# A fourth quad per gate/up block: one low by an adding DMA, carried blocks in f32, and a head that starts from x already turned

## The chip, the cores and the metric

One core of a Trainium2 chip runs the kernel. The metric is the device time of one execution in microseconds (us). All inputs lie in DRAM at the start, and the output must lie there at the end. PE is TensorE, DVE is VectorE, ACT is ScalarE, POOL is GpSimd, and SP is SyncE, whose queue starts the weight loads.

## The reference

One layer over 256 tokens of width 2048, all in f32:

```python
h = x
f = swiglu(rmsnorm(h, ln_ffn1_pre), ffn1_gate, ffn1_up, ffn1_down)
h = h + 0.5 * rmsnorm(f, ln_ffn1_post)
mx = hybrid_mixer(rmsnorm(h, ln_mix_pre), w_in, rwkv..., pool..., w_proj_a, w_proj_b, w_out)
h = h + rmsnorm(mx, ln_mix_post)
f = swiglu(rmsnorm(h, ln_ffn2_pre), ffn2_gate, ffn2_up, ffn2_down)
h = h + 0.5 * rmsnorm(f, ln_ffn2_post)
# swiglu(x, g, u, d) = (silu(x @ g) * (x @ u)) @ d, with g, u 2048 x 5632 and d 5632 x 2048
# hybrid_mixer: p = u @ w_in (2048 x 8480); a WKV-7 scan branch and a pooling branch,
#   each projected to 2048, gated by sigmoids of p, added, and multiplied by w_out
```

## The kernel before

**Products.** Every f32 product is made of three f32r matmuls (mm3): each operand is split into a high part (an ACT cast) and a low part (a DVE subtraction), and high·high, high·low and low·high are summed in PSUM. A step of 128 rows of the weight (a k) against 128 tokens (a half h) and 512 columns is one mm3.

**The plan.** Most of the work is put in order by a small planner in the kernel's own code. `job` notes a piece of work with its engine, an assumed duration and a due time; `pe` notes a piece for PE; `run` calls `play`, which runs through time by these assumptions and issues each engine's earliest due piece. So the order on PE, ACT and DVE is written out when the kernel is built, and each engine follows it in order. Weight buffers are limited: `take` and `give` pass on four w buffers (f32 weights, tag w32) and five pairs of wH and wL (tag ws). A pool of 33 units of 4 KB per partition holds everything larger.

**Gate and up.** The 5632 columns of gate and up are worked off in 11 blocks of 512. Blocks 0 and 1 take plain products. Blocks 2 to 10 (list FAST) go through `seven`, which computes gate (f) and up (l) together from a string of letters. An f or l is a *pair*: two k of one weight against both halves, 12 matmuls, fed by `feed` (SP loads w, ACT casts wH, DVE subtracts wL). A q is a *quad*: two k of both weights at once by a scheme of seven products in place of eight, 21 matmuls, for which DVE makes sums of the weights (t13, t24 at L513 to L521) and their lows (L534), and for which sums S1 to S4 of the activations are made once (`sums`). `merge`, `plus` and `total` add the banks up (L570). The result is multiplied with silu of the gate, turned in 32x32 squares on DVE (`turn`, L786), and carried to its place by 16 small POOL DMAs (`carry`, L797); then ACT and DVE split it into high and low (L809, L813) for the down product.

**Down and post.** `post` multiplies the carried blocks with w_down, by the lists DOWN (with 7 and 8 quads) in both FFNs, and by OUT in the mixer, then normalises and adds the residual. For its quads `sums` first joins high and low of a carried block (join, L394).

**Head.** `head` starts the kernel: 12 turns (matmuls against the identity) warm PE; x comes in by rows, PE turns each 128x512 piece (`turn4`, L768), ACT and DVE split it, and the first gate product follows between the turns. The gain of the first norm is turned on PE too (L1781), and `setup_mixer` loads 11 parameter vectors as rows and turns them (L1152).

**Mixer.** Its first column block is begun in the plan (`lead`) and ended outside of it (`gemm_rest`). Its middle lies outside the plan, with PE's order written by hand (`weave`); w_proj_a's product at its end is in `pair_g` and `gemm_tok`.

Of the kernel before, what the change touches and what calls it, by code (L numbers as in the profile page):

```python
# [11 lines left out]
F32 = mybir.dt.float32  # L12
# [28 lines left out]
WARM = 12  # L41
# [5 lines left out]
FAST = {b: "fffqffqllqlll" for b in range(2, 11)}  # L47
# [7 lines left out]
ROWS = [("ln_mix_pre", 16), ("ln_ffn2_pre", 16), ("mu", 26), ("w0", 8), ("a0", 8),  # L55
        ("k_k", 8), ("k_a", 8)]
ROWS2 = [("r_k", 8), ("gn_w", 8), ("gn_b", 8), ("pool_scale", 8)]
# [18 lines left out]
class Block:  # L76
# [43 lines left out]
    def job(s, eng, dur, fn, due=0.0, deps=(), take=None, give=(), lag=None,  # L120
            rel=0.0):
        s.n += 1
        n = Node(s.n, eng, dur, fn, due, LAG[eng] if lag is None else lag, give)
        n.ready = rel if eng != "D" else rel - 10
        for d in deps:
            s.link(d, n)
        if take:
            s.asks.setdefault(take, []).append(n)
        if eng != "P":
            s.jobs.append(n)  # L130
        return n
# [14 lines left out]
    def run(s):  # L146
# [3 lines left out]
        for name, ns in s.asks.items():  # L150
            ns.sort(key=lambda n: n.due)
            wait[name] = deque(ns[CAPS[name]:])
            for n in wait[name]:
                n.left += 1
        order = deque(n for _, n in sorted(s.order, key=lambda o: o[0]))
        with s.tc.manual_schedule(engines={E.PE, E.Activation, E.DVE}):
            s.play(order, wait)
            s.stats()
        s.clk, s.order, s.asks, s.freed, s.jobs = 0.0, [], {}, {}, []

    def play(s, order, wait):

        free = dict(P=0.0, A=0.0, V=0.0, G=0.0, D=-10.0)
# [17 lines left out]
        def done(n, t):  # L181
            for name in n.give:
                if wait.get(name):
                    met(wait[name].popleft(), t)
            for k in n.kids:
                met(k, t)
# [81 lines left out]
    def feed(s, w, k, n, c0, t, hold=False):  # L268
# [3 lines left out]
        def get():  # L272
            b["w"] = s.get_w(w, k, n, c0, 512)

        def high():
            if hold:
                b["H"], b["L"] = s.unit(dt=F32R, p="kH"), s.unit(dt=F32R, p="kL")
            else:
                b["H"], b["L"] = [s.wp.tile([P, 1024], F32R, tag=g, name=s.nm(g), bufs=WS_BUFS)
                                  for g in ("wH", "wL")]  # L280
            s.nc.scalar.copy(b["H"][:, :m], b["w"][:, :m])  # L281
# [4 lines left out]
        def low():  # L286
            s.nc.vector.tensor_tensor(out=b["L"][:, :m], in0=b["w"][:, :m],  # L287
                                      in1=b["H"][:, :m].bitcast(F32), op=ALU.subtract)
        g = s.job("D", 1.75 * m / 1024, get, t - 9, take="w")
        h = s.job("A", aa(m), high, t - va(m) - aa(m) - 0.5, (g,), None if hold else "ws")  # L290
        return b, s.job("V", va(m), low, t - va(m) - 0.3, (h,), give=("w",))
# [10 lines left out]
    def gemm(s, w, c0, at, k0, k1, KT, evac, names, kd=lambda k: (), pss=None):  # L302
# [9 lines left out]
        for k in range(k0, k1, 2):  # L312
            b, l = s.feed(w, k, 2, c0, s.clk)
            e = s.pe(12 * MM, lambda k=k, b=b: do(k, b),
                     (l, *kd(k), *kd(k + 1), *(s.open(*names) if k == 0 else ())), ("ws",))
# [4 lines left out]
    def halves(s, w, c0, at, k0, k1, KT, names, pss, kd=lambda k, h: (), ends=None):  # L320

        fed, last = {}, None
        for k in range(k0, k1, 2):
            fed[k] = s.feed(w, k, 2, c0, s.clk + (k - k0) * 3 * MM, k - k0 >= 2 * WS_BUFS)
        for h in range(2):
            for k in range(k0, k1):
                b, l = fed[k // 2 * 2]

                def do(k=k, h=h, b=b):
# [3 lines left out]
                last = s.pe(3 * MM, do, (l, *kd(k, h), *(s.open(names[h]) if k == 0 else ())),  # L333
                            ("ws",) if h and k % 2 and k - k0 < 2 * WS_BUFS else ())
# [3 lines left out]
    def gemm_tok(s, w, c0, at, KT, evac, xs=None):  # L338

        pss = [s.pm.tile([P, 512], F32, tag="mm", name=s.nm("mm")) for _ in range(2)]  # L340
        ws = {}

        def do(k, h):
            (wH, wL), (xH, xL) = ws[k], at(k)
            s.mm3(pss[h], xH[:, h * P:h * P + P], xL[:, h * P:h * P + P], wH, wL,
                  k == 0, k == KT - 1)

        def keep(tiles):
            ws.update((k, (wH, wL)) for k, wH, wL in tiles)

        if xs:
            s.head(w, c0, KT, do, keep, xs)
        else:
            for k2 in range(0, KT, 4):
                keep(s.load_w(w, k2, min(4, KT - k2), c0, 512))
                for k in range(k2, min(k2 + 4, KT)):
                    do(k, 0)
                    do(k, 1)
        with s.tc.high_priority(offset=BOOST):
            for h in range(2):  # L360
                evac(h, pss[h])

    def lead(s, w, c0, at, KT, kd):
# [3 lines left out]
        s.run()  # L367
        return pss

    def gemm_rest(s, w, c0, at, KT, evac, pss):  # L370

        for k2 in range(STAG, KT, 4):
            ws = {k: t for k, *t in s.load_w(w, k2, min(4, KT - k2), c0, 512)}
            for k in range(k2, min(k2 + 4, KT)):
                for h in range(2):
                    (wH, wL), (xH, xL) = ws[k], at(k)
                    s.mm3(pss[f"f{h}"], xH[:, h * P:h * P + P], xL[:, h * P:h * P + P],
                          wH, wL, k == 0, k == KT - 1)
        with s.tc.high_priority(offset=BOOST):
            for h in range(2):  # L380
                evac(h, pss[f"f{h}"])

    def sums(s, src, sm, q0, nq, t, deps, own=None, hl=False):
# [12 lines left out]
        def four():  # L396
            x = tt["x"] if hl else src[j][:, q0 % 2 * 2:][:, :2 * nq].rearrange(
                "p (i b) t -> p i b t", b=2)
            a11, a21 = x[:, :, 0, :P], x[:, :, 0, P:]
            a12, a22 = x[:, :, 1, :P], x[:, :, 1, P:]  # L400
            f = tt["f"] = s.unit((P, 4, nq, P), F32, "sf")
            V.scalar_tensor_tensor(out=f[:, 0], in0=a21, scalar=-1.0, in1=a22, op0=ALU.mult,
                                   op1=ALU.subtract)
            V.scalar_tensor_tensor(out=f[:, 1], in0=f[:, 0], scalar=-1.0, in1=a11,
                                   op0=ALU.mult, op1=ALU.subtract)
# [3 lines left out]
        def parts():  # L409

            for n_ in ("sH", "sL"):
                if j % 2 == 0:
                    own["12" + n_] = s.unit((P, 2, 2, 2, P), F32R, n_)
                if j % 4 == 0:
                    own["4" + n_] = s.unit((P, 4, 2, P), F32R, n_)
            s3 = [u.rearrange("p (i b) t -> p i b t", b=2)[:, :, 0, P:] for u in src[j]]
            s12, s4 = [[own[m + n_] for n_ in ("sH", "sL")] for m in ("12", "4")]
# [27 lines left out]
        if hl:  # L445
            deps = (s.job("V", va(512 * nq), join, t - 6, deps, rel=t - 16),)
        a = s.job("V", 4 * va(P * nq), four, t - 4.5, deps)
# [10 lines left out]
    def seven(s, wf, cf, wl, cl, at, KT, sm, order, ev_first, ev_last, trail=0,  # L458
# [26 lines left out]
        def pair(k, w, c0, b):  # L485
            ws, l = s.feed(w, k, 2, c0, s.clk)

            def do():
# [4 lines left out]
                12 * MM, do, (l, *kd(k), *kd(k + 1), *banks(b + "0", b + "1")), ("ws",))  # L493
            return e

        def quad(q):
            k = 2 * q
            v, x = {}, {}
            t1 = s.clk
            t2, t3, t4 = [t1 + m * MM for m in (6, 9, 15)]  # L500

            def get(n_, *tiles):
                v[n_] = t = s.wp.tile([P, 1024], F32, tag="w32", name=s.nm("w32"),
                                      bufs=W32_BUFS).rearrange("p (a c) -> p a c", a=2)
# [19 lines left out]
            def split(n_, m, t, deps, give=()):  # L524
                def high():
                    wH, wL = [s.wp.tile([P, 1024], F32R, tag=g, name=s.nm(g), bufs=WS_BUFS)
                              for g in ("wH", "wL")]
                    x[n_] = [t_[:, :m * 512].rearrange("p (a c) -> p a c", a=m)
                             for t_ in (wH, wL)]
                    nc.scalar.copy(x[n_][0], v[n_])  # L530

                def low():
# [4 lines left out]
                h = s.job("A", aa(w_), high, t - va(w_) - aa(w_) - 0.5, deps, "ws")  # L537
                return s.job("V", va(w_), low, t - va(w_) - 0.3, (h,), give=give)
            ga = s.job("D", 1.75, lambda: get("a", (k, wl, cl), (k + 1, wf, cf)), t1 - 9, (), "w")
            gb = s.job("D", 1.75, lambda: get("b", (k, wf, cf), (k + 1, wl, cl)), t2 - 9, (), "w")  # L540
# [5 lines left out]
            s.job("N", 0, None, 0, (la, j2), give=("w",))  # L546
            s.job("N", 0, None, 0, (lb, j4), give=("w",))
# [6 lines left out]
                 (la, *dep, *banks("p1", "f0")), ("ws",))  # L554
            s.pe(3 * MM, lambda: mul("l0", rows(k + 1, 0), x["b"][0]),
                 (lb, *banks("l0")), ("ws",))
            s.pe(6 * MM, lambda: (mul("p5", S_(1), x["t13"][0]),
                                  mul("p7", S_(3), x["t13"][1])),
                 (l13, *banks("p5", "p7")), ("ws",))
            return s.pe(6 * MM, lambda: (mul("p6", S_(2), x["t24"][0]),  # L560
                                         mul("l1", rows(k + 1, 1), x["t24"][1])),
                        (l24, *banks("p6", "l1")), ("ws",))
        u = []
# [5 lines left out]
        def add(o, b, i):  # L569
            V.tensor_tensor(out=u[o], in0=pss[b], in1=u[i], op=ALU.add)  # L570
# [4 lines left out]
        def merge(e, t):  # L575
            j0 = s.job("A", 0.5, start, t, (e,), "u")
# [10 lines left out]
        for c in order:  # L587
# [5 lines left out]
            else:  # L593
                last[c] = pair(next(ks[c]), *wc[c], c)
# [12 lines left out]
        if trail:  # L607
# [4 lines left out]
            s.halves(wl, cl, at, KT - trail, KT, KT, ("l0", "l1"), pss, lambda k, h: kd(k), end)  # L612
# [5 lines left out]
        s.job("N", 0, None, 0, fin, give=("u",))  # L618
        return use

    def head(s, w, c0, KT, do, keep, xs):

        load, turn = xs
        w32 = {}
# [4 lines left out]
        def split(k):  # L629
            n, t = w32[k]  # L630
            keep(s.two(t, k, n, 512))
        E = mybir.EngineType
        with s.tc.manual_schedule(engines={E.PE, E.Activation, E.DVE, E.SP}):
            ps = s.psum("warm")
            for _ in range(WARM):
                s.nc.tensor.transpose(ps[:, :P], s.ident, s.ident)
            load(0, 0)
            load(1, 0)
            load(None, None)
# [1215 lines left out]
```

## Time and profile before

| | |
|---|---|
| median of 3 runs | 2032.9 us (2032.25 to 2036.04) |
| the profiled execution | 2033.49 us |
| its span, first to last instruction | 2031.8 us |
| PE busy | 2014.8 us, 99% |
| DVE busy | 1735.4 us, 85% |
| ACT busy | 1164.7 us, 57% |
| POOL busy | 326.6 us, 16% |
| DMA | 423.55 MB, mean 208 GB/s |

The profile was taken in one execution. A row of a view names the line of the kernel, the engine, the operation and the tiles it writes and reads; "x61" is a count, and behind the bar stand the busy time, the mean duration of one in ns, and the idle time of the engine just before it with what ended it. In the timeline a row begins with the start and the duration in us; in square brackets stands the idle time before it. In the table by stretches, each engine has its busy time and the number of its instructions, and at the end stand the granted clock, the share of the DMA engines and GB/s. PE's matmuls overlap: the duration of one is longer than the distance to the next.

### The profile page before, as it was taken

The numbers are of one execution on the slowest core, as the hardware profiler recorded it, in microseconds if no ns is written. First come the engines' busy times: TensorE is split into PE (matmuls) and PEld (weight loads), VectorE is DVE, ScalarE is ACT, GpSimd is POOL, SyncE is SP. The second block draws the span as 40 slices with busy tenths as digits, with TensorE's granted clock in tenths as the row PEclk, the third lists the DMA queues.
The fourth block names the chain that finished last, engine by engine and source line by source line (L and its number), as shares of the span: only waits on it lengthen the run. The fifth ranks groups of instructions, "written<-read, shape, count | busy, mean of one in ns | idle before, by whom it ended". The sixth has DMA issues, their size and how long they took to land.

```text
span 2031.8 us, 28759 instructions
## 1 busy us (share of the span) xinstructions
PE 2014.8 (99%) x10011; PEld 1664.1 (82%) x10011; DVE 1735.4 (85%) x2300; ACT 1164.7 (57%) x1559; POOL 326.6 (16%) x673
## 2 busy tenths in 40 slices
PE   9999999999999999999999999999999999999997
PEld 7888888888888888888788788888888878888886
DVE  6989999988998857789689577769999989989986
ACT  7555565555565566685575444565565555555653
POOL 0121112211000023403220111012211122110000
PEclk9999999999999999999999999999999999999999
DMA  7666676766667777757456557676666767666674
GB/s 261 205 198 218 217 220 203 226 201 221 208 207 253 233 210 215 205 176 215 144 176 183 161 171 271 209 219 192 213 211 216 222 190 232 201 221 209 205 258 146
DMA packets 226842, 423.55 MB, mean 208 GB/s; under 512 B 24063, under 2 KB 27529, under 8 KB 226697
## 3 DMA queue, kind: packets, MB, share of 16 engines
q1 hardware_dynamic: 204137, 384.70, 60.8%
q0 software_dynamic: 22272, 36.51, 5.5%
q8 instruction: 78, 1.28, 0.3%
q10 hardware_dynamic: 288, 0.52, 0.1%
q14 instruction: 67, 0.55, 0.1%
HBM read 396.69 MB, written 8.39 MB: 199 GB/s over the span
## 4 chain that ended last, share of the span: by engine, by line
PE 97%; issue 1%; DMA 1%; DVE 1%; ACT 1%; POOL 0%; DVEq 0%; POOLq 0%; SPq 0%; ACTq 0%
PE mm L264 27%; PE mm L266 27%; PE mm L265 27%; PE ms L266 4%; PE ms L265 4%; PE ms L264 4%; PE tr L768 1%; DMA x<-T 0%; PE pA L1575 0%; PE mc L728 0%; PE pU L1671 0%; DMA w<-in_ffn_gate_dram 0%; PE pSa L1683 0%; PE pY L1706 0%; PE pT L1742 0%
## 5 line engine op out<-in xcount | busy, mean ns | idle before, releaser
L264 PE MATMUL mm<-wH,xH 128*128 128x512 f32 (+1 forms) x2232 | 871.6, 391 | 0.0
L266 PE MATMUL mm<-wH,xL 128*128 128x512 f32 (+1 forms) x2232 | 866.5, 388 | 0.6 <-DVE xL L777 0.5
L265 PE MATMUL mm<-wL,xH 128*128 128x512 f32 (+1 forms) x2232 | 866.6, 388 | 0.2
L281 ACT CAST wH<-w 128x1024 fp32r<-128x1024 f32 x373 | 388.1, 1053 | 231.3 <-PE mm L266 139.5
L287 DVE TENSOR_TENSOR wL<-w,wH 128x1024 fp32r<-128x1024 f32 x373 | 449.4, 1221 | 77.8 <-ACT wH L281 72.0
L266 PEld LDWEIGHTS mm<-wH,xL 128*128 128x128 f32 x2232 | 419.0, 188 | 87.9 <-DVE xL L777 2.3
L264 PEld LDWEIGHTS mm<-wH,xH 128*128 128x128 f32 x2232 | 419.1, 188 | 86.4 <-ACT xH L772 0.2
L265 PEld LDWEIGHTS mm<-wL,xH 128*128 128x128 f32 x2232 | 419.3, 188 | 85.1 <-DVE wL L287 1.0
L530 ACT CAST wH<-t 128x1024 fp32r<-128x1024 f32 x172 | 181.1, 1053 | 221.9 <-DVE t L521 113.1
L797 POOL DMA_DIRECT2D x<-T x352 | 173.1, 499 | 735.2 <-issue 299.0
L241 DVE TENSOR_TENSOR wL<-w,wH 128x1024 fp32r<-128x1024 f32 (+3 forms) x178 | 209.9, 1188 | 82.7 <-ACT wH L240 81.2
L240 ACT CAST wH<-w 128x1024 fp32r<-128x1024 f32 (+3 forms) x178 | 182.1, 1027 | 149.7 <-PE mm L266 129.3
L534 DVE TENSOR_TENSOR wL<-t,wH 128x1024 fp32r<-128x1024 f32 x172 | 205.9, 1219 | 14.3 <-ACT wH L530 13.6
L530 ACT CAST wH<-w 128x1024 fp32r<-128x1024 f32 (+1 forms) x172 | 143.1, 834 | 70.7 <-PE mm L266 32.5
L534 DVE TENSOR_TENSOR wL<-w,wH 128x1024 fp32r<-128x1024 f32 (+1 forms) x172 | 163.7, 952 | 5.2 <-ACT wH L530 5.0
L513 DVE TENSOR_TENSOR t<-w,w 128x1024 f32<-128x1024 f32 x86 | 105.0, 1220 | 12.2 <-DMA w<-in_ffn_down_dram 7.6
L570 DVE TENSOR_TENSOR u<-mm,u 128x512 f32<-128x512 f32 x92 | 61.1, 683 | 11.0 <-PE mm L266 11.0
L265 PE MATMUL ms<-wL,sH 128*128 128x512 f32 x174 | 67.9, 390 | 1.4 <-DVE wL L534 1.4
L264 PE MATMUL ms<-wH,sH 128*128 128x512 f32 x174 | 67.8, 390 | 1.0 <-ACT wH L530 1.0
L266 PE MATMUL ms<-wH,sL 128*128 128x512 f32 x174 | 67.7, 389 | 0.0
L570 DVE TENSOR_TENSOR u<-ms,u 128x512 f32<-128x512 f32 x92 | 61.3, 687 | 1.6
L809 ACT CAST xH<-x 128x512 fp32r<-128x512 f32 x44 | 26.8, 617 | 62.4 <-DMA x<-T 59.5
(332 smaller groups left out, 2064.4 us busy)
## 6 DMA issues: line engine op xcount, KB each, us to landing
w<-in_w_in_dram SPq DMA_DIRECT2D x128, 512.0 KB
w<-in_ffn_up_dram SPq DMA_DIRECT2D x122, 512.0 KB
w<-in_ffn_gate_dram SPq DMA_DIRECT2D x120, 512.0 KB
w<-in_ffn_down_dram SPq DMA_DIRECT2D x116, 512.0 KB
w<-in_ffn_down_dram SPq DMA_DIRECT2D x120, 256.0 KB
w<-in_ffn_gate_dram SPq DMA_DIRECT2D x112, 256.0 KB
w<-in_ffn_up_dram SPq DMA_DIRECT2D x108, 256.0 KB
w<-in_w_out_dram SPq DMA_DIRECT2D x28, 512.0 KB
```

What stands on the lines that cost most here:

```text
L240: s.nc.scalar.copy(vH, v)
L241: s.nc.vector.tensor_tensor(out=vL, in0=v, in1=vH.bitcast(F32), op=ALU.subtract)
L264: nc.tensor.matmul(ps, aH, bH, start=start, stop=False)
L265: nc.tensor.matmul(ps, aH, bL, start=False, stop=False)
L266: nc.tensor.matmul(ps, aL, bH, start=False, stop=stop)
L281: s.nc.scalar.copy(b["H"][:, :m], b["w"][:, :m])
L287: s.nc.vector.tensor_tensor(out=b["L"][:, :m], in0=b["w"][:, :m], in1=b["H"][:, :m].bitcast(F32), op=ALU.subtract)
L513: V.tensor_tensor(out=v["t13"], in0=v["a"], in1=v["b0"].to_broadcast([P, 2, 512]), op=ALU.subtract)
L530: nc.scalar.copy(x[n_][0], v[n_])
L534: V.tensor_tensor(out=L, in0=v[n_], in1=H.bitcast(F32), op=ALU.subtract)
L570: V.tensor_tensor(out=u[o], in0=pss[b], in1=u[i], op=ALU.add)
L797: nc.gpsimd.dma_start(out=x[0][q * 32:q * 32 + 32, i], in_=src[i * 32:i * 32 + 32, q])
```

## The change

FAST goes from 3 quads and 10 pairs to 4 quads and 8 pairs per block, in blocks 2 to 10 of both FFNs. A capital letter marks a pair whose low is made another way (`feed_add`): ACT writes −w, rounded as wH is, to wL, and a POOL DMA adds w onto it in place; DVE has no part in it:

```diff
-FAST = {b: "fffqffqllqlll" for b in range(2, 11)}
+WARM = 26
+AHEAD = 9.0
+MORE=(dict(w=(400,)*2, ws=(400,)*3), dict(w=(550,)*2, ws=(550,)*3))
+FAST = {b: "Ffqffqlqqlll" for b in range(2, 11)}

+    def feed_add(s, w, k, c0, t):
+        b = {}
+        def get():
+            b["t"] = s.get_w(w, k, 2, c0, 512, b["w"] is not None)
+        def high():
+            b["H"], b["L"] = s.room(b["ws"] is not None)
+            s.nc.scalar.copy(b["H"], b["t"])
...
+        def minus():
+            s.nc.scalar.activation(out=b["L"], in_=b["t"], func=AF.Copy, scale=-1.0)
+        def add():
+            s.nc.gpsimd.dma_start(out=b["L"], in_=b["t"], accum_op=ALU.add)
+        g = s.job("D", 1.75, get, t - AHEAD - 9, take=("w", b))
+        h = s.job("A", aa(1024), high, t - AHEAD, (g,), ("ws", b))
+        m = s.job("A", aa(1024), minus, t - AHEAD + 0.1, (h,))
+        a = s.job("G", 0.93, add, t - AHEAD + 1.5, (m,), lag=0.0)
+        return b, s.job("D", 3.2, lambda: None, t - AHEAD + 2, (a,), give=(("w", b),))
```

MORE lends the plan units as further buffers, two for w and three pairs for wH and wL, up to 400 us of planned time in FFN1 and 550 us in the plan that holds FFN2.

The carried blocks stay in f32 (list hX, one unit each in place of two): `carry` ends with the DMAs, the split into high and low becomes a job of `post`, due just ahead of the block's first use, and `sums` reads hX without a join. The S sums use plain adds and subtractions, with the sign of S1 turned, and their tiles are kept under a block number:

```diff
+        if hX is not None:
+            return s.job("N", 0, None, 0, ms)
+        return s.split(lambda: x[0], hT, b, t + 10.5, (ms,))
...
+            for b, t in sorted(first.items(), key=lambda a: a[1]):
+                hj[b] = s.split(lambda b=b: hX[b], hT, b, t - (8.5 if b * 2 < n else 2.5),
+                               ((xj[b],),), t - 22)
```

The host lays x out a second time with its 2048 columns on the partitions (x_t) and all parameter vectors as columns (cols). `head` loads x_t, splits each k with one ACT and one DVE instruction of 256 columns, and warms PE with 26 turns; x by rows is loaded after that, for the statistics of the first norm alone:

```diff
-            turn(0, 0)
-            split(1)
-            turn(1, 0)
...
+        def part(k):
+            H, L = [u[:, k % 4] for u in uT[k // 4]]
+            v = xT[k // 4][:, k % 4]
+            nc.scalar.activation(out=H, in_=v, func=AF.Copy, scale=g[:, k:k + 1])
+            nc.vector.scalar_tensor_tensor(out=L, in0=v, scalar=g[:, k:k + 1],
+                                           in1=H.bitcast(F32), op0=ALU.mult,
+                                           op1=ALU.subtract)
```

In the mixer `lead` now holds its whole column block, and w_proj_a's product, its gating and its turns (`plan_pa`) become jobs of the second plan, which counts ACT and DVE as taken for its first 3 us. The norms' statistics are jobs too (`stat`). The scan's tile t11 is laid out by group.

627 lines of the change are left out of this document (314 added, 313 removed).

## The prediction

> **What bounds the kernel now.** I read the page first.
>
> ```profile
> span 2031.8 us, 28759 instructions
> PE 2014.8 (99%) x10011; PEld 1664.1 (82%) x10011; DVE 1735.4 (85%) x2300; ACT 1164.7 (57%) x1559; POOL 326.6 (16%) x673
> PE 97%; issue 1%; DMA 1%; DVE 1%; ACT 1%; POOL 0%; DVEq 0%; POOLq 0%; SPq 0%; ACTq 0%
> ```
>
> PE is busy 99% of the span and carries 97% of the chain that ended last. So time falls only if PE executes fewer instructions or waits less. The busy times by stretch show what a gate/up block costs (the first row has the head and blocks 0 and 1, 138 to 388 us lies in blocks 3 to 8, the third row is in the down product):
>
> ```profile
> 0.00:98.00 98.00, 95.58 (x430) 78.45 (x431) 75.28 (x112) 61.80 (x102) 12.23 (x52) 1.00 0.72 233
> 138.00:388.00 250.00, 250.00 (x1104) 207.09 (x1103) 238.25 (x272) 145.42 (x166) 47.15 (x96) 1.00 0.69 215
> 475.00:697.00 222.00, 222.00 (x981) 183.80 (x981) 195.90 (x230) 124.61 (x146) 12.09 (x24) 1.00 0.68 221
> ```
>
> 1104 matmuls in 250 us: one of 512 columns costs 0.2266 us of PE. The third busy column, DVE, has 238.25 of 250 us, 95%: there the next bound is close. ACT has 58%, DMA 0.69.
>
> **The change, part by part.** *The fourth quad.* A quad does with 21 matmuls what two pairs do with 24. A block goes from 3×21 + 10×12 = 183 matmuls (41.5 us) to 4×21 + 8×12 = 180 (40.8 us). Nine blocks in each of two FFNs: 18 × 3 × 0.2266 = 12.2 us less PE. What this costs DVE comes from the timeline, where one quad's work stands in line:
>
> ```profile
> 152.26 1.22 DVE L513 TENSOR_TENSOR t<-w,w 128x1024 f32<-128x1024 f32 x1
> 153.40 1.22 DVE L534 TENSOR_TENSOR wL<-w,wH 128x1024 fp32r<-128x1024 f32 x1
> 154.53 0.68 DVE L517 TENSOR_TENSOR t<-w,t 128x512 f32<-128x512 f32 x1
> 155.13 0.68 DVE L534 TENSOR_TENSOR wL<-w,wH 128x512 fp32r<-128x512 f32 x1
> 155.74 0.68 DVE L521 TENSOR_TENSOR t<-w,t 128x512 f32<-128x512 f32 x1
> 156.34 1.22 DVE L534 TENSOR_TENSOR wL<-t,wH 128x1024 fp32r<-128x1024 f32 x1
> ```
>
> Start to start, 1024 columns take 1.14 us and 512 take 0.60. A quad is four of the first (t13 and three lows) and three of the second: 6.36 us. A pair's low is 1.14. Beside them a block has 8 sums of banks, 2 products and 2 turns (512 columns each), and today 2 lows of a carried block. Before: 19.1 + 11.4 + 14×0.60 = 38.9 us; the row above gives 0.953 × 41.5 = 39.5, so 0.6 us are bubbles. After: 4×6.36 + 7×1.14 (the F pair's low goes to a DMA) + 12×0.60 = 40.6 us, or 41.2 with the bubbles, against 40.8 us of PE. DVE goes from 95% to about 100% of PE's time.
>
> Whether PE then waits depends on DVE's idle time. Today, in 138 to 388 us:
>
> ```profile
> L287 DVE TENSOR_TENSOR wL<-w,wH 128x1024 fp32r<-128x1024 f32 x61 | 73.6, 1221 | 6.2 <-ACT wH L281 4.5
> L534 DVE TENSOR_TENSOR wL<-t,wH 128x1024 fp32r<-128x1024 f32 x36 | 42.9, 1220 | 1.3 <-ACT wH L530 1.2
> L513 DVE TENSOR_TENSOR t<-w,w 128x1024 f32<-128x1024 f32 x18 | 22.0, 1220 | 1.8 <-DMA w<-in_ffn_gate_dram 1.7
> L813 DVE TENSOR_TENSOR xL<-x,xH 128x512 fp32r<-128x512 f32 x12 | 8.3, 688 | 2.1 <-ACT xH L809 2.1
> ```
>
> 11.75 us of idle in six blocks, 1.95 each. The L287 part is mostly full buffers (its casts wait for PE to free wH), which is slack and not a cost; L813's goes with the carried lows. 1.3 and 1.8 us stay, 0.5 per block. So DVE falls behind by between 0 and 0.9 us a block (40.6 to 41.2, plus 0 to 0.5, less 40.8). Nine blocks make 0 to 8 us per FFN, 0 to 16 in all. Against it stand the stock of ready weights at the start of block 2 (five wH/wL buffers, now up to eight with MORE; one is 2.7 us of PE in a pair) and the two extra w buffers. I take 1.5 us of waits per FFN, +3 in all: near the low end, because the first blocks and the down product leave DVE room to fill and empty the stock. The sums for the fourth quad are made once per FFN, in blocks 0 and 1, where DVE has 75 of 98 us.
>
> ```profile
> L281 ACT CAST wH<-w 128x1024 fp32r<-128x1024 f32 x373 | 388.1, 1053 | 231.3 <-PE mm L266 139.5
> ```
>
> ACT gets 1.5 casts more per quad than per two pairs, and the F pair's negation of the same size: 2.6 us a block at this row's 1.05, less the two carried highs, on 17 us of idle per block. Hidden.
>
> *Carried blocks in f32.* Their high/low splits leave the gate/up blocks. Today these make PE wait twice, once per FFN:
>
> ```profile
> 409.09 0.62 ACT L809 CAST xH<-x 128x512 fp32r<-128x512 f32 x1 [5.57 <-DMA x<-T]
> 410.91 0.40 PE L264 MATMUL ms<-wH,sH 128*128 128x512 f32 x1
> 411.98 0.50 PE L265 MATMUL ms<-wL,sH 128*128 128x512 f32 x1 [0.67 <-DVE wL L534]
> 414.05 0.40 PE L266 MATMUL mm<-wH,xL 128*128 128x512 f32 x1
> 1643.95 0.62 ACT L809 CAST xH<-x 128x512 fp32r<-128x512 f32 x1 [6.86 <-DMA x<-T]
> 1644.22 0.39 PE L266 MATMUL ms<-wH,sL 128*128 128x512 f32 x1
> 1645.57 0.50 PE L264 MATMUL ms<-wH,sH 128*128 128x512 f32 x1 [0.96 <-ACT wH L530]
> 1648.90 0.40 PE L266 MATMUL mm<-wH,xL 128*128 128x512 f32 x1
> ```
>
> ACT stood 5.6 and 6.9 us at a cast whose carry DMA was late, with the quad's wH casts behind it. From 410.91 to 414.05 lie 8 matmul steps (1.81 us) in 3.14; from 1644.22 to 1648.90 lie 9 (2.04) in 4.68: 1.3 + 2.6, 4.0 us lost, which go. The splits come back at the down product, 9 blocks × 2 × 0.60 = 10.8 us of DVE less four joins (4×1.14), 6 us on its 26 us of idle in 222: hidden if the carries have landed, and all but the last two have had a block's time.
>
> *The adding transfer.* One 512 KB DMA from POOL in each of 18 blocks, issued by plan 7.5 us ahead of the pair that needs it. No such add is in the trace; the nearest are POOL's plain transfers:
>
> ```profile
> x<-T POOLq DMA_DIRECT2D x352, 32.0 KB, 3.9
> h<-hsp POOLq DMA_DIRECT2D x8, 512.0 KB, 9.2
> gb<-in_ln_ffn_post_dram POOLq DMA_DIRECT2D x4, 512.0 KB, 5.7
> xr<-in_x_dram POOLq DMA_DIRECT2D x4, 512.0 KB, 6.7
> ```
>
> 5.7 to 9.2 us for the size. At 5.7 or 6.7 it lands before PE asks (cost 0, my value: h and xr are issued four at once and share the engines, gb stands nearly alone); at 9.2 it is 1.7 us late, 18 × 1.7 = 31 us. It queues on POOL behind carry moves only if a carry is late; ACT's casts are in front of it and ACT has room. [...]
>
> *The head.* The rows, in order of time:
>
> ```profile
> 1.72 2.82 PE L636 MATMUL warm<-ident 128*128 128x128 f32 x12 [1.72 <-POOL ident masks.py:199]
> 5.62 0.62 ACT L240 CAST wH<-w 128x512 fp32r<-128x512 f32 x1 [2.60 <-DMA w<-in_ffn_gate_dram]
> 5.99 1.12 PE L768 MATMUL tr<-ident,x 128*128 128x128 f32 x4 [0.18 <-DMA x<-in_x_dram]
> 6.75 0.78 PE L264 MATMUL mm<-wH,xH 128*128 128x512 f32 x1
> 22.51 0.60 PE L768 MATMUL tr<-ident,x 128*128 128x128 f32 x4
> 22.86 0.48 PE L264 MATMUL mm<-wH,xH 128*128 128x512 f32 x1
> 23.18 0.39 PE L265 MATMUL mm<-wL,xH 128*128 128x512 f32 x1
> 33.12 0.40 PE L264 MATMUL mm<-wH,xH 128*128 128x512 f32 x1
> ```
>
> The 96 matmuls of gate block 0 run from 6.75 to 33.12, 26.4 us for 21.8 us of work. Six groups of four turns stand between them (22.51 to 23.18 is 0.67 for 0.23: 0.44 each, 2.6); 1.9 are waits and slow first matmuls. With x coming in already turned, both go, but for 0.3 I keep. The start hangs on the first weight (5.62) and on 26 warming turns in place of 12. In these rows a turn takes 0.21 us as late as 6.5 us ((2.82−0.42)/11; four in 1.12), so 26 of them from 1.72 would end at 7.3 if none is faster; with the later half at twice the speed, 5.9. I take 6.8, near the slow rows. 6.8 + 21.8 + 0.3 = 28.9: 4.2 us gained, 3.7 to 5.1. [...] The two turns by which setup_mixer brings its gain columns to the partitions go too (0.1 us each by the spacing of late turns, 0.44/4). The gains and the first step of x go out on ACT's queue, the rest of x on SP's between the weights. The x rows for the statistics (2 MB more) queue on SP behind x and w, ahead of block 0's up weights.
>
> ```profile
> 2.00:24.00 22.00, 21.31 (x100) 17.03 (x100) 13.87 (x33) 14.43 (x37) 1.74 (x22) 1.00 1.02 366
> ```
>
> Loads run at 366 GB/s in these 22 us; x, w, x again and the first up weights are 8.5 MB, 23 us, so they are there before 29: hidden. A step k needs 384 KB in 1.36 us of PE, 289 GB/s: also covered.
>
> *The rest.* lead's remainder and the w_proj_a product move from the tile scheduler into the plan: the same matmuls, turns and DMAs in another order, POOL's msp loads 25 to 30 us ahead of their use. The S sums by plain adds, tiles kept by block number, statistics as planned jobs and the other layout of t11 keep the number and width of their instructions; normed in FFN1 has one scaling of x in place of an add and a product, in blocks 0 and 1 on DVE's room. PE's chain has 97% of the span, so there is little to win in all of this, and I cost it 0; the nearest bound for a loss is one late ACT cast, 1.3 to 2.6 us (above).
>
> Sum, against this execution's own 2033.5 us (span 2031.8; 0.6 over the median 2032.9): 2033.5 − 12.2 − 4.0 − 4.2 − 0.2 + 3 = 2015.9, say **2016**.
>
> **The rivals.** *DVE becomes the bound.* The stock does not help and DVE's shortfall, 0.5 to 0.9 us a block, is paid by PE in full: waits of 8 to 16 us in all, 2012.9 + 8 to 16, so 2021 to 2029. If DVE kept today's whole idle of 1.95 us, a block would take 42.6 to 43.2 us, over the 41.5 of now, and the time would be 2033.5 − 8.4 + 18 × 1.1 to 1.7, 2045 or more. For it: the 95% above; no row shows DVE held at 100% for long. Against: most of today's idle is full buffers.
>
> *The add is late (the other side).* Each F pair opens its block, so a late landing stops PE at once, and quads behind it give no slack. Every microsecond of lateness costs 18. It decides at 17.5/18 = 1.0 us late, a landing 8.5 us after issue; at 9.2 us the time is 2016 + 31 = 2047. For it: the h row, the destination that must be read as well as written, 0.69 DMA share. Against: gb and xr rows, and ACT's room to issue earlier.
>
> *The carry stall only moves.* The splits wait at the head of the down product for late carries and stop ACT there as at 1644: 4 us or twice that again, 2020 to 2024.
>
> **How the numbers follow.** Forecast (PE still the bound, waits of 0 to 8 us, 2011 to 2021): 0.60. DVE the bound: 0.22 (0.18 for 2021 to 2029, 0.01 within 0.2% of before, 0.03 above). Add late: 0.09 (0.08 slower, 0.01 no change). Carry stall moved: 0.09. A measurement of this kernel tells 0.2%, 4 us, from no change. Faster 0.60 + 0.18 + 0.09 = 0.87; same 0.02; slower 0.11. The range: down to 2010 (no waits give 2012.9, the head's best another 0.9, the rest the run's own spread of 2 us), up to 2028, nearly all of the DVE case. Left out: the rest of it, the late add and a little below, 0.18.
>
> **What would show it.** Right: 512-column matmuls down by 54; gate block 0's 97th such matmul near 29 us; no ACT wait on a carry DMA before the down product; gate/up blocks of 40.8 us with DVE at 97% or more; PE's waits there under 8 us. Wrong: PE waiting at a block's first pair on a DMA (the add); PE waiting on wL all through the blocks (DVE); long ACT waits after 460 us (the carries).

## The result and the profile after

The changed kernel takes 2014.4 us (median of 4 runs, 2014.3 to 2015.2), the kernel before 2032.6 beside it: ratio 0.9908, interval 0.9891 to 0.9925. The profiled execution has a span of 2012.8 us, 19.0 less than before. The top of its page, with the chain by engine:

```profile
span 2012.8 us, 28601 instructions
PE 1997.0 (99%) x9936; PEld 1651.9 (82%) x9936; DVE 1764.8 (88%) x2362; ACT 1200.2 (60%) x1599; POOL 339.8 (17%) x689
...
PE 97%; DVE 1%; issue 1%; ACT 1%; DMA 0%; SPq 0%; POOL 0%; DVEq 0%; POOLq 0%; ACTq 0%
```

PE is still the bound. Busy time by stretch (length, then PE, PEld, DVE, ACT, POOL with their counts, granted clock, DMA share, GB/s): head with blocks 0 and 1; six gate/up blocks of FFN1; the down product; the nine blocks of FFN2, but for the first 8 us and with the first 9 of its down product.

```profile
0.00:96.00 96.00, 93.52 (x412) 77.95 (x413) 74.08 (x105) 62.54 (x88) 12.89 (x51) 1.00 0.83 286
135.00:385.00 250.00, 250.00 (x1104) 207.07 (x1104) 248.97 (x291) 151.84 (x172) 52.75 (x102) 1.00 0.76 236
463.00:700.00 237.00, 237.00 (x1055) 196.31 (x1054) 216.89 (x274) 141.48 (x190) 15.73 (x30) 1.00 0.68 223
1412.00:1780.00 368.00, 368.00 (x1625) 304.84 (x1624) 360.96 (x421) 228.76 (x263) 76.64 (x150) 1.00 0.72 223
```

DVE is busy 248.97 of 250 us, 99.6%, and PE waits for nothing in that stretch: 250.00 busy. The view of PE's waits for the whole execution is short (us in total, times, longest):

```profile
PE warm L649 <- POOL ident masks.py:199: 1.7, 1, 1.7
PE mm L274 <- DVE wL L250: 0.8, 1, 0.8
PE pS L1712 <- ACT R L1706: 0.7, 1, 0.7
PE mm L275 <- DVE xL L759: 0.3, 1, 0.3
```

The splits of the carried blocks, in the groups of ACT, first before and then after the change (the last columns are ACT's idle time ahead of them and its releaser):

```profile
L809 ACT CAST xH<-x 128x512 fp32r<-128x512 f32 x44 | 26.8, 617 | 62.4 <-DMA x<-T 59.5 <-DVE wL L534 2.9
```

```profile
L803 ACT CAST xH<-x 128x512 fp32r<-128x512 f32 x44 | 25.4, 615 | 1.0 <-issue 1.0
```

44 casts either way; ACT stood 59.5 us at them for carry DMAs, and no longer does.

The 19.0 us come apart so. 54 matmuls of 512 columns fewer are recorded (8328 for 8382): 12.2. Call it a gap when the starts of two such matmuls lie further apart than 0.227 us, and count what is over. These gaps fell by 1.35 us in 400 to 450 and by 2.67 in 1600 to 1650, the places of the two carry stalls: 4.0. The head, to the 97th such matmul (30.51 for 33.12): 2.6. Together 18.8. The shares are read off the two traces by place; no run puts the carried blocks or the head back alone.

### The profile page after: what moved, and what is told of

The parts are those of the page before. It is cut to its first block, busy times and chain, and to the rows that moved or that the text cites. A ratio compares the mean times of both kernels' runs of the same rounds, so it can differ in the third digit from the quotient of the medians.

```text
span 2012.8 us, 28601 instructions
## 1 busy us (share of the span) xinstructions
PE 1997.0 (99%) x9936; PEld 1651.9 (82%) x9936; DVE 1764.8 (88%) x2362; ACT 1200.2 (60%) x1599; POOL 339.8 (17%) x689
## 3 DMA queue, kind: packets, MB, share of 16 engines
HBM read 398.79 MB, written 8.39 MB: 202 GB/s over the span
## 4 chain that ended last, share of the span: by engine, by line
PE 97%; DVE 1%; issue 1%; ACT 1%; DMA 0%; SPq 0%; POOL 0%; DVEq 0%; POOLq 0%; ACTq 0%
PE mm L273 27%; PE mm L275 26%; PE mm L274 26%; PE ms L275 5%; PE ms L274 5%; PE ms L273 5%; PE pA L1596 0%; PE tr L750 0%; DMA w<-in_ffn_gate_dram 0%; PE mc L732 0%; DVE fg L1052 0%; PE pU L1692 0%; DVE wL L298 0%; DVE xL L759 0%; PE pSa L1704 0%
## 5 line engine op out<-in xcount | busy, mean ns | idle before, releaser
L273 PE MATMUL mm<-wH,xH 128*128 128x512 f32 (+1 forms) x1711 | 668.8, 391 | 0.0
L274 PE MATMUL mm<-wL,xH 128*128 128x512 f32 (+1 forms) x1711 | 663.2, 388 | 0.8 <-DVE wL L250 0.8
L275 PE MATMUL mm<-wH,xL 128*128 128x512 f32 (+1 forms) x1711 | 663.4, 388 | 0.3 <-DVE xL L759 0.3
L292 ACT CAST wH<-w 128x1024 fp32r<-128x1024 f32 x251 | 262.6, 1054 | 174.8 <-PE mm L275 122.9
L298 DVE TENSOR_TENSOR wL<-w,wH 128x1024 fp32r<-128x1024 f32 x251 | 301.3, 1218 | 58.3 <-ACT wH L292 56.7
L250 DVE TENSOR_TENSOR wL<-w,wH 128x1024 fp32r<-128x1024 f32 (+2 forms) x159 | 188.2, 1192 | 74.4 <-ACT wH L249 73.0
L249 ACT CAST wH<-w 128x1024 fp32r<-128x1024 f32 (+2 forms) x159 | 162.7, 1027 | 135.6 <-PE mm L275 113.6
L273 PE MATMUL mm<-kH,xH 128*128 128x512 f32 x449 | 175.5, 391 | 0.0
L275 PE MATMUL mm<-kH,xL 128*128 128x512 f32 x449 | 174.9, 389 | 0.0
L274 PE MATMUL mm<-kL,xH 128*128 128x512 f32 x449 | 174.7, 389 | 0.0
```

The lines of the kernel that those rows point to most:

```text
L249: s.nc.scalar.copy(vH, v)
L250: s.nc.vector.tensor_tensor(out=vL, in0=v, in1=vH.bitcast(F32), op=ALU.subtract)
L273: nc.tensor.matmul(ps, aH, bH, start=start, stop=False)
L274: nc.tensor.matmul(ps, aH, bL, start=False, stop=False)
L275: nc.tensor.matmul(ps, aL, bH, start=False, stop=stop)
L292: s.nc.scalar.copy(b["H"][:, :m], b["t"][:, :m])
```

## Experiments: what lets DVE run full without PE waiting

Two theories for the gate/up blocks. One: DVE's work, 40.6 us in a block of 40.8, just fits, the spare wH/wL pairs level out the rest, and the F pair's transfer is needed to make it fit. The rival: the stock gained in the first blocks carries a DVE that is too slow, and the lent buffers matter little.

**Four quads alone.** The kernel before with only the new list, its F written as a plain pair:

```diff
-FAST = {b: "fffqffqllqlll" for b in range(2, 11)}
+FAST = {b: "ffqffqlqqlll" for b in range(2, 11)}
```

> The kernel before with four quads and eight plain pairs in blocks 2 to 10 and nothing else of the change (carried blocks split in the gate/up blocks, no adding transfer, no lent buffers, old head). Theory: DVE's work per block is 40.6 + 1.14 + 2 x 0.60 = 43.0 us, 2.2 over PE's, 20 us per FFN, of which a stock of 4 to 8 us is saved: 2032.6 - 12.2 + 24 to 32, so 2044 to 2052, slower than before. Rival (quads pay by themselves): 2020 to 2022.

Measured 2082.0 us, ratio 1.0241 (1.0225 to 1.0256): the right direction, several times the size. Its blocks 3 to 8 and PE's longest waits:

```profile
135.00:385.00 250.00, 243.55 (x1047) 194.34 (x1046) 249.23 (x290) 146.17 (x168) 46.90 (x96) 1.00 0.67 209
```

```profile
PE mm L265 <- DVE wL L534: 17.1, 34, 1.5
PE ms L265 <- DVE wL L534: 11.8, 42, 0.9
```

1047 matmuls in 250 us make 43.0 us for a block of 180. DVE's work there is 40.6 + 1.14 (the F pair's low) + 1.20 (two carried lows) = 42.9. So here DVE is the bound, and PE pays the difference from the start; the stock that I had credited was not there. The shortage runs on into the last block, which alone has 6.8 us of gaps, and into the down product from 494 us on, with 3.8.

**The F pair by DVE, all else as changed.**

```diff
-FAST = {b: "Ffqffqlqqlll" for b in range(2, 11)}
+FAST = {b: "ffqffqlqqlll" for b in range(2, 11)}
```

> The changed kernel, but the first pair of each block takes its low on DVE again (F becomes f, no adding transfer). Theory (PE's instructions set the time as long as DVE's work per block is under PE's 40.8 us; what is over is paid, less a stock of ready weights): DVE is busy 243.97 of 245 us in blocks 3 to 8 of the changed kernel, 40.6 us per block; with 1.14 more it is 41.8, 1.0 over PE, 9 us per FFN. With 4 to 8 us of stock 1 to 5 us per FFN are paid: 2016 to 2024, with PE waiting on DVE late in the gate/up blocks. Rival (DVE's load is not the limit, the add is not needed): 2014 to 2015. Second rival (no stock): 2032.

Measured 2024.8 us, 0.9967 (0.9954 to 0.998). Blocks 3 to 8, and PE's waits:

```profile
135.00:385.00 250.00, 249.83 (x1101) 206.36 (x1100) 249.51 (x289) 144.74 (x163) 46.99 (x96) 1.00 0.67 213
```

```profile
PE tr L750 <- DVE sga L1352: 4.7, 1, 4.7
PE ms L274 <- DVE wL L534: 2.1, 7, 0.6
```

DVE is full (99.8%) and PE still hardly waits up to 341 us: the stock lasts for six blocks. In the last three PE loses 0.7, 0.9 and 1.8 us, and 0.5 behind them: 3.9 us in FFN1 and 4.2 in FFN2. That is the theory's stock, seen at work, and the add's worth in the blocks: 8 us. The wait of 4.7 from 1224 us on lies far from the blocks, at w_proj_a's turns; that the list alters the order of the second plan there is my reading. The granted clock is 0.50 for 6.8 us about it (1225.96 to 1232.78), and this execution took 2028.0 us, 3.2 over the median. Nothing in my theories had that.

**No buffers lent.**

```diff
-        s.run(MORE[0])
+        s.run()
...
-        s.run(MORE[1], 3.0)
+        s.run({}, 3.0)
```

> The changed kernel without the lent buffers (MORE empty in both plans; four w buffers and five wH/wL pairs throughout). Theory: DVE's work is just under PE's in a block, so no deep stock is needed: 2014 to 2018. Rival (the lent buffers are what lets DVE run at 100% without PE waiting): 2020 or more, with PE waits spread over the blocks.

Measured 2076.6 us, 1.0214 (1.0198 to 1.023): 62 us over the changed kernel. My theory fell. Its blocks, with DVE's largest idle group:

```profile
135.00:385.00 250.00, 241.00 (x1037) 192.65 (x1036) 237.87 (x275) 144.53 (x161) 51.76 (x101) 1.00 0.71 217
```

```profile
L298 DVE TENSOR_TENSOR wL<-w,wH 128x1024 fp32r<-128x1024 f32 x39 | 47.1, 1220 | 12.0 <-ACT wH L292 12.0
```

DVE is no longer full: it stands 12.0 us at lows whose casts are late, while PE waits for those lows. That a DVE with this much to do is not the bound but is itself starved was in neither theory. Two kinds of buffer were taken away at once, so each was then lent alone.

**The three pairs alone**, without the two staging buffers w:

```diff
-MORE=(dict(w=(400,)*2, ws=(400,)*3), dict(w=(550,)*2, ws=(550,)*3))
+MORE=(dict(ws=(400,)*3), dict(ws=(550,)*3))
```

> The changed kernel with only the three extra wH/wL pairs lent in the gate/up blocks, and not the two extra staging buffers w (both kinds lent: 2014.4 us; neither: 2076.6). Theory (an F pair holds its w from the load to the landing of its add, some 20 us, and takes it from the four others, so that loads come late): most of the 62 us come back, 2045 to 2075, with ACT waiting on the DMA of w and DVE waiting on ACT. Rival (the three pairs are what carries DVE's shortfall): 2014 to 2025.

Measured 2083.4 us, 1.0255 (1.0235 to 1.0275): the pairs by themselves bring nothing (7 us more than with nothing lent). The blocks, and ACT's idle time there, which names what is missing:

```profile
135.00:385.00 250.00, 235.12 (x1011) 190.60 (x1010) 231.56 (x268) 142.40 (x159) 51.81 (x101) 0.99 0.70 211
```

```profile
L530 ACT CAST wH<-w 128x512 fp32r<-128x512 f32 (+1 forms) x36 | 28.2, 797 | 25.0 <-DMA w<-in_ffn_up_dram 14.6 <-DMA w<-in_ffn_gate_dram 8.8 <-PE ms L275 1.5
...
L292 ACT CAST kH<-w 128x1024 fp32r<-128x1024 f32 x21 | 21.9, 1047 | 16.1 <-DMA w<-in_ffn_up_dram 15.5 <-DMA w<-in_ffn_gate_dram 0.5
L292 ACT CAST wH<-w 128x1024 fp32r<-128x1024 f32 x17 | 17.9, 1051 | 13.0 <-DMA w<-in_ffn_up_dram 11.9 <-DMA w<-in_ffn_gate_dram 1.2
```

Over 50 us of ACT's time in six blocks go on weights that have not come, at a DMA share of 0.70, less than the 0.76 at which the changed kernel has no waits: not the rate of the DMA engines holds them, but loads that start late for want of a buffer. ACT's wait alone would not say so: with four quads alone it waits some 36 us for weights too, while DVE is full. Here DVE is not: it is busy 231.56 of 250 us.

**The two w alone** (and, in the same kernel, the head's third load halved; that part is told below):

```diff
+MORE=(dict(w=(400,)*2), dict(w=(550,)*2))
```

> The changed kernel with two edits that act in different stretches of the trace. In the head: the weights of k = 2 and 3 as two loads of 256 KB with casts and lows of their own, and 22 warming turns, without the tiny loads (the up weight stays first on SP's queue). In the gate/up blocks: only the two extra staging buffers w lent, and not the three extra wH/wL pairs (pairs alone gave 2083 us). Head, theory (the stall at 10.3 to 11.5 us comes from the arrival and the splitting of one load of 1024 columns; the mended order before this one only lost its gain by late up weights): first matmul at 6.7 to 7.2, no stall over 0.3 us before the up block, 97th matmul at 29.0 to 29.6; rival (a later weight stalls instead): 30.0 or later. Blocks, theory (the two w buffers are what the F pair takes away, and a stock of ready pairs is not needed): no waits of PE on wL between 96 and 460 us, 2012.8 to 2013.6 in all; rival (the pairs are the stock that carries a DVE at 99.6%): waits of PE on wL of 1 to 2 us a block, 2025 to 2050.

Measured 2026.5 us, 0.9969 (0.9957 to 0.998). Blocks 3 to 8 and the main wait:

```profile
135.00:385.00 250.00, 248.95 (x1092) 204.21 (x1091) 246.60 (x288) 155.69 (x171) 52.71 (x102) 1.00 0.76 232
```

```profile
PE ms L274 <- DVE wL L534: 3.0, 10, 0.5
```

With w alone the blocks lose 9 us over both FFNs (4.3 and 5.0 more between starts than in the changed kernel), about half a microsecond a block. Of the other 3 us over the changed kernel most lie at 1200 to 1250 (1.8) and in the altered head (0.3). So of the lent buffers the two w are worth some 50 us (2076.6 to 2026.5, with the altered head in it) and the three pairs, on top of them, some 9. Both theories had a part of it: the pairs carry a shortfall of the size that I had worked out (0.5 to 0.9 a block), and without the w there is nothing to carry. An F pair keeps its w from its load to the landing of its add, which may be why two more are needed; no run tries that by itself. The first run of this section points the same way: with plain pairs and four w buffers DVE was full (249.23) at 43.0 us a block, and in the changed kernel with nothing lent it stood idle (237.87) at 43.4. But those two differ in the carried blocks and the head as well.

**The old list in the changed kernel.**

```diff
-FAST = {b: "Ffqffqlqqlll" for b in range(2, 11)}
+FAST = {b: "fffqffqllqlll" for b in range(2, 11)}
```

> The changed kernel with the old list of three plain quads and ten plain pairs in blocks 2 to 10; head, f32 carried blocks and lent buffers stay. Theory: 54 matmuls of 0.2266 us come back, 12.2 us, and nothing else: 2026.6, within 1. Rival (part of the gain comes from elsewhere or the quads cost something): more than 1.5 us off that, under 2025 or over 2028.

Measured 2033.8 us, 1.0006 (0.9996 to 1.0015), 7 over the forecast and no faster than the kernel before: span 18.9 over the changed kernel's. 12.2 of it is the quads. New waits of PE hold the rest, and they eat up what the head and the carried blocks had gained:

```profile
PE tr L750 <- DVE sga L1352: 3.1, 1, 3.1
...
PE ms L274 <- DVE wL L534: 1.5, 1, 1.5
...
PE mm L274 <- DVE wL L298: 0.7, 1, 0.7
```

The last two and the matmuls about them cost 3.3 us at 1814 to 1820, early in the down product of FFN2, which begins near 1788; the first costs 3.1 up to 1229, and 1.3 more in slower matmuls behind it. The carry stalls at 411 and 1644 are not there, so the changed kernel is without them under either list.

**Eight quads in the down product.** Two pairs of its first column group made a quad:

```diff
-DOWN = ((0, "fffffffffqffffqfflqlllqllqllqllqlllll", 0),
+DOWN = ((0, "ffffffffqffffqffqlqlllqllqllqllqllll", 0),
```

> The changed kernel with an eighth quad in the first column group of each down product (one quad for two pairs: 3 matmuls of 512 columns less, twice): 6 x 0.2266 = 1.36 us less PE; DVE has idle time there (217 of 237 us busy). Theory (PE is the bound there and the quad's lows hide): 2013.1, 8322 matmuls of 512 columns recorded for 8328. Rival (the changed list shifts the plan's order and opens waits elsewhere, as with the other lists tried): 2014.4 or more, with the waits named in PE's view.

Measured 2014.8 us, 0.991 (0.9896 to 0.9923). The six matmuls went (8322 recorded), and the profile shows a new wait at 536.6 us:

```profile
536.58 0.50 PE L274 MATMUL ms<-wL,sH 128*128 128x512 f32 x1 [1.20 <-DVE wL L534]
```

With what is around it, it costs 2.0 us for 1.4 gained. The rival had it; the 0.4 us between the medians lies within the spread of the runs.

**A shorter lead for the adds.**

```diff
-AHEAD = 9.0
+AHEAD = 3.0
```

> The changed kernel with the planned lead of the adding transfers cut by 6 us (AHEAD 9.0 to 3.0). In the changed kernel the adds were issued 11 to 12 us ahead of the F pair that reads them and took 6.7 to 7.3 us to land, so the slack is about 4 to 5 us. Theory (the add costs nothing only because it is issued early; each us of lateness costs 17 to 18 us over the two FFNs): issued some 5.5 us ahead, it lands 1.2 to 1.8 us late at each of 17 blocks, 20 to 31 us in all, 2035 to 2046 us, with waits of 1 to 2 us of PE on kL or wL at the first pair of the blocks. Rival one (PE's order holds other ready work, or the plan's engines still run ahead of their due times): within 0.2% of 2014. Rival two (the later lead also frees the w buffer and the wH/wL pair later, or earlier, so that DVE's supply shifts): waits on wL in the midst of the blocks rather than at their first pair.

Measured 2020.7 us, 0.9942 (0.9927 to 0.9956), 6 over the changed kernel: outside the theory and outside the first rival, but nearer to the rival. The adds go out only 2 to 5 us later, since ACT runs ahead of its due times. The answer on the add's line (its landings), first of the changed kernel and then of this one, with PE's wait on it:

```profile
DMA to landing us min/median/max: 5.4/7.0/9.2
```

```profile
DMA to landing us min/median/max: 5.1/8.1/9.8
```

```profile
PE mm L274 <- DMA wL<-w: 0.4, 1, 0.4
```

One add, issued at 331.73 us, took 9.8 us, and PE stood at its low until 341.55. In the changed kernel the adds are issued 11 to 12 us ahead (124.72 for a pair that PE reaches at 136.9), so 9.2 does no harm; the landings spread wider than the 6.7 to 7.3 of the expectation. Here the lead is 8 to 10 in the blocks after the first, and the slowest just shows. Of the 6 us, 2.3 lie in the mixer (850 to 900) and 1.8 at 1800 to 1850, in FFN2's down product, away from the adds, and 0.7 at this one.

## Experiments: the head

The head gained 2.6 us and not 4.2. The changed kernel's rows, in order of time:

```profile
0.81 0.44 SPq L235 DMA_DIRECT2D w<-in_ffn_up_dram  x1
...
1.30 0.47 SPq L235 DMA_DIRECT2D w<-in_ffn_gate_dram  x1
...
1.72 5.81 PE L649 MATMUL warm<-ident 128*128 128x128 f32 x26 [1.72 <-POOL ident masks.py:199]
...
7.18 0.71 PE L273 MATMUL mm<-wH,xH 128*128 128x512 f32 x1
...
9.17 1.05 ACT L249 CAST wH<-w 128x1024 fp32r<-128x1024 f32 x1 [0.83 <-DMA w<-in_ffn_gate_dram]
...
10.27 0.50 PE L273 MATMUL mm<-wH,xH 128*128 128x512 f32 x1
...
11.53 0.50 PE L274 MATMUL mm<-wL,xH 128*128 128x512 f32 x1 [0.76 <-DVE wL L250]
...
30.51 0.39 PE L273 MATMUL mm<-wH,xH 128*128 128x512 f32 x1
```

The first load on SP's queue is an up weight that PE wants at 30 us; the 26 turns hold PE to 7.2; the third weight (k = 2 and 3, one load of 512 KB) lands at 9.17, its low is ready at 11.5, and PE loses 1.0 us there. Theories: the up weight, the turns, or the loads as a whole.

**Tiny loads to hold the up weights back**, ahead of the loads of the columns and of x by rows, with 26 turns and then with 20:

```diff
+            for _ in range(W32_BUFS):
+                hold = s.wp.tile([P, 1024], F32, tag="w32", ...)
+                nc.sync.dma_start(out=hold[:, :8], in_=s.cols_in[:, :8])
             x(None, None)
```

> The changed kernel with four tiny loads (8 columns each) put into the four staging buffers of weights in the head, so that no up weight can be fetched ahead of the first gate weights; in the changed kernel one up weight of 512 KB, wanted at 30 us, was the first load on SP's queue. Theory (that load holds up the first gate weights and causes the second stall of 0.5 us at 11.5 us): the first gate weight lands 0.5 to 1.2 us earlier; the first matmul stays at 7.2, since the 26 warming turns end at 7.3, but the stall at 11.5 goes, and the 97th matmul of 512 columns starts near 29.9 instead of 30.5: 2013.8. Rival (the engines share bandwidth and the up weight costs the head nothing): 97th matmul at 30.4 to 30.6, 2014.4.

> The same as the run before it, with 20 warming turns in place of 26. Theory (with the first gate weight there earlier, the 26 turns at 0.21 us are what holds the first matmul): turns end at 1.72 + 20 x 0.213 = 6.0, the first matmul starts at 6.0 to 6.4, and the 97th at 28.9 to 29.3, which is what was forecast for the head; 2012.9. Rival (the first weight is the bound, or fewer turns leave the first matmuls at half rate): 97th matmul at 29.9 or later.

Measured 2018.5 us, 0.9932 (0.9918 to 0.9947), and 2020.0 us, 0.9936 (0.9922 to 0.9951). First matmul at 6.12 and 5.88. The up weight did hold the start: the kernel with eight quads has the changed head, its turns sped up as early as here (4.89 us, here 5.01), and it starts at 6.93, on a cast:

```profile
6.93 0.50 PE L273 MATMUL mm<-wH,xH 128*128 128x512 f32 x1 [0.62 <-ACT wH L249]
```

In the changed kernel's own execution no turn sped up, and there the turns hold it to 7.18. But the third weight was cast at 9.06 and 8.69, PE stood at the same place, and the 97th matmul came at 34.30 and 35.19. The tiny loads wait for their buffers on SP, and everything behind them waits too. In the kernel with 20 turns they are issued from 11.32 to 15.65 us, and the load of the columns goes out at 16.66, in the changed kernel at 11.54:

```profile
21.63 0.18 DVE L1155 TENSOR_SCALAR omu<-cols 128x27 f32<-128x27 f32 x1 [5.27 <-DMA cols<-in_cols_dram]
...
23.06 0.80 PE L274 MATMUL mm<-wL,xH 128*128 128x512 f32 x1 [3.54 <-DVE wL L250]
```

A small DVE instruction on the late columns held the weights' lows behind it. What these two tested is thus mixed with a stall of their own.

**12 turns.**

```diff
-WARM = 26
+WARM = 12
```

> The changed kernel with 12 warming turns, as before the change, in place of 26. Theory (the turns' number decides how fast the first matmuls of 512 columns run, and 26 of them also hold the first one up): the turns end at 4.3, the first matmul starts when its low is there, 6.7 to 6.8, and the first four or five matmuls take 0.34 to 0.58 us from start to start, as before the change, in place of 0.23, 0.8 to 1.0 us lost: 97th matmul at 30.5 to 31.0, 2014.4 to 2015. Rival (PE's rate after a pause of 2.4 us stays at half for some 3.4 us of work): 1.7 us lost and 0.4 won, 31.8, 2015.7.

Measured 2015.2 us, 0.9915 (0.9898 to 0.9932), 97th matmul at 30.53. The first matmul starts at 6.51; eight run at half rate (0.427 us from start to start, over 3.41 us at a granted clock of 0.50); and the block ends where it did with 26 turns, because the stall at the third weight takes up what they lost. The runs that leave the head as it is say the same: over the changed kernel and six of them the first matmul starts between 6.76 and 7.19 and the 97th between 30.26 and 30.63. The turns are not what the head hangs on.

**The third weight in two halves**, the tiny loads behind columns and x, 20 turns:

```diff
-            get(2, 2)
+            get(2, 1)
+            get(3, 1)
...
             split(2)
             part(3)
+            split(3)
```

> The changed kernel with the head's loads in another order: the four tiny loads that keep up weights away now stand behind the loads of the columns and of x (where they held nothing else up), the weights of k = 2 and 3 come as two loads of 256 KB with two casts and two lows of 512 columns in place of one of 1024, and 20 warming turns. Theory (the head is bound by the arrival and splitting of its third weight, which came at 8.7 to 9.2 us in all four orders run so far and reached PE, low included, at 11.0 to 11.5): landing half a load earlier (0.6 us), a cast of 0.62 for 1.05 and a low of 0.69 for 1.22, so the stall before 11.5 us shrinks from 1.0 to between 0 and 0.3; the first matmul starts near 6.0, the 97th at 28.5 to 29.3 in place of 30.5: 2012.4 to 2013.2. Rival (the loads as a whole are too slow: the stall only moves to the next weights): 97th at 30.0 to 30.5, 2014 to 2014.4.

Measured 2018.6 us, 0.9929 (0.9915 to 0.9942). Gate block 0 does end earlier, its 96th matmul starting at 29.43 where the changed kernel has 30.28; then the up weights, which queue behind the tiny loads (issued from 21.37 on, for 18.44), are not there:

```profile
29.43 0.39 PE L275 MATMUL mm<-wH,xL 128*128 128x512 f32 x1
31.81 0.50 PE L273 MATMUL mm<-wH,xH 128*128 128x512 f32 x1 [2.00 <-ACT wH L292]
33.07 0.50 PE L274 MATMUL mm<-wL,xH 128*128 128x512 f32 x1 [0.76 <-DVE wL L298]
```

With the up weight first again (the two-w kernel above, 22 turns) the 97th matmul starts at 30.85: the stall only moves to k = 4, whose weights land at 12.22. In the changed kernel the DMA share over this stretch is

```profile
0.00:31.20 31.20, 28.72 (x126) 24.29 (x127) 18.67 (x30) 19.08 (x30) 2.79 (x32) 1.00 0.97 358
```

Every order tried gave the first microsecond back to a load that came later. That the loads as a whole are the head's bound fits all of it; a head with fewer bytes, which would show it, was not run. No version here beats the changed kernel.

## Why the prediction came out right, point by point

- *The fourth quad, −12.2:* 54 matmuls fewer, blocks of 40.8 us, as worked out; with the old list the kernel loses another 7 us to waits in the mixer and in FFN2's down product, which the sum had not. DVE's 40.6 us a block held: 248.97 busy in 250.
- *New PE waits, +3 (0 to 16):* measured 0. DVE's bubbles, which I had at up to 1.1 us a block from the idle time before, shrank to 0.17 (1.03 in 6.1 blocks); with nothing lent they are 2.1 (12.13 in 5.8). I had put the levelling down to the stock of pairs; the runs put some 9 us on the pairs and some 50 on the w, which I had named in half a sentence.
- *Carried blocks, −4.0:* 4.0, and ACT waits on no carry DMA at all. The rival that the stall moves to the down product did not happen.
- *The adding transfer, 0:* right in the sum, though not by the reason first given. The planned lead of 7.5 us would have been short of some landings (5.4 to 9.2); the real lead was 11 to 12, for the reason that I gave second, ACT's room to issue earlier. The rows from which I priced it are medians, and I left out one of the same size, `gb<-in_ln_mix_post_dram` at 10.2; single h transfers took up to 13.8. By the planned lead those would have been late; that no add was rests on the real lead, which the sum had not sized. There the value 0 had luck.
- *The head, −4.2 (3.7 to 5.1):* 2.6; the mis-sized step. The start came at 7.18 for 6.8, at the slow end: no turn of this execution ran at full rate (each took 0.21 us), as one may or may not (last section). Behind it lie 1.6 us of waits and slow matmuls for 0.3: I had called the loads covered because their mean rate (366 GB/s) was above the need (289), and did not ask when the third weight would land.
- *The rest, 0:* the gaps between 600 and 1400 us make 104.6 us before and 103.6 after, and the end behind the last matmul of 512 columns grew by 1.1: in sum nothing.
- *Sum:* 2015.9 forecast for this execution, 2014.5 measured: waits 3 too high, the head's end 1.6 too early. The two misses partly cancel, so the sum is nearer than its terms.

## What to carry to other kernels

Where the second engine is as full as the bound, ask what keeps it fed before how much stock it has: here two staging buffers decided 50 us and three ready pairs 9. A transfer that holds its source until it lands takes that buffer out of turn (the adds here for 5 to 9 us), so price the buffer with the transfer; how much of the 50 us comes from that is not shown. And check a start by when each load lands, one by one, rather than by the mean rate.

## What the runs showed of the hardware

PE's half rate could be seen switching. In the kernel with 12 turns, four stretches of 3.41 us:

```profile
1.22:4.63 3.41, 2.82 (x12) 2.42 (x12) 0.29 (x1) 1.49 (x2) 2.20 (x25) 1.00 0.71 221
4.63:8.04 3.41, 1.31 (x4) 0.86 (x5) 2.04 (x4) 2.61 (x5) 0.00 (x0) 1.00 1.02 375
8.04:11.45 3.41, 3.41 (x10) 2.64 (x8) 2.05 (x4) 1.88 (x4) 0.00 (x0) 0.50 1.04 400
11.45:14.86 3.41, 3.41 (x16) 2.82 (x15) 2.78 (x6) 3.31 (x6) 0.00 (x0) 1.00 1.04 395
```

After 3.41 us in which PE was busy 1.31, the next 3.41 ran at a granted clock of 0.50, though PE was by then busy throughout: eight matmuls of 0.427 us each. (The 1.00 of the first row is no measurement: the trace's clock record begins at 4.60, and the turns before that take 0.213 us each, the half rate.) A stretch with 1.70 us busy (26 turns and tiny loads, 8.39 to 11.80) was followed by 0.51 as well, one with 2.21 (eight quads, 533.96 to 537.37) by 1.00.

The half rate lasted 3.41 us there; with the F pair by DVE it lasted 6.82 (1225.96 to 1232.78), twice that. The full rate of the changed kernel, from 7.68 to 2004.48 us, is 585 times 3.413. So the same can be counted in all 14 traces, in stretches of 3.413 us from the first change of each trace's clock on. All 11 stretches at full rate with PE busy 1.62 us or less were followed by one at half rate; of 14 with 1.64 to 1.91 us, 2 were; of more than 8000 with 1.93 or more, one was (2.43, four quads alone, from 5.37 us). In these traces, then, the clock fell almost only after stretches in which PE was busy for less than about half. At the start a stretch with 2.67 us busy (the kernel before, 0.98 to 4.39) did not bring the full rate, one with 2.82 (12 turns, 1.19 to 4.60) did.

The clock first rose between 4.60 us (12 turns) and 7.81 us (the kernel before) over the 14 traces, a spread of 3.2 us. Of the eight traces with 26 turns, three, the changed kernel's among them, have no turn at full rate (0.11 us), and in five the last ones are. So the head has a part that differs from one execution to the next, whatever the number of turns.
